# RMS norm on one core: the second tile stored in 4, 4 and 24 rows, the third loaded in one transfer

## The chip, the cores and the metric

The kernel runs on one core of one Trainium2 chip. The metric is the device time of one execution in microseconds (us), here the median of several. The core has engines that work beside each other: TensorE (PE in the profile), VectorE (DVE), ScalarE (ACT), GpSimd (POOL) and SyncE (SP). Each takes its instructions in order and waits on semaphores for the others. Transfers between memory (HBM) and the on-chip memory (SBUF) are issued by an engine's queue, here SP's and ACT's, and are carried out by 16 DMA engines that all queues share. In the profile SP's transfers are q1 and ACT's are q10.

## The reference

```python
def reference(x, gamma):          # x: 16 x 1024 x 512 fp32, gamma: 512 fp32
    eps = 1e-5
    rms = np.sqrt(np.mean(x ** 2, axis=-1, keepdims=True) + eps)
    return (x / rms * gamma).astype(np.float32)
```

There are 16,384 rows of 512 numbers. 33.55 MB are read and 33.55 MB are written, and for each number there is one square, one addition and two multiplications.

## The kernel before

**Tiles.** The rows are cut into four tiles of 4,096. A tile lies on 128 partitions with 32 rows each, so one row of a tile is 2 KB on a partition and 0.26 MB in all, and a whole tile is 64 KB on a partition and 8.39 MB in all. A partition's rows lie one behind the other in HBM too, so a transfer of n rows moves one unbroken run of 2n KB for each partition. There are three slots for tiles: tiles 0, 1 and 2 get slots 0, 1 and 2, and tile 3 uses slot 0 again, so its loads wait until tile 0 has been stored.

**Groups.** Each tile is worked on in two groups of 16 rows, (0, 0), (0, 16), (1, 0) and so on to (3, 16), as the list `groups` has them. In a group ScalarE squares pieces of 7, 5 and 4 rows (7 and 9 in tile 0; line 105) and VectorE sums each piece (line 106). `inverse_rms` makes 1/rms with a square root on ScalarE (line 111) and a reciprocal on VectorE (line 112). GpSimd then scales the last rows of the group (six, seven or three, `share`) and multiplies them by gamma (lines 118 and 119). ScalarE scales the other rows one by one (line 127), and VectorE multiplies these by gamma in one instruction (line 131, in `times_gamma`). The pieces of nine rows in tile 0 put their squares into rows 23 to 31 of slot 2, since nothing has been loaded there yet.

**Order.** The schedule is written by hand: each engine runs its instructions in program order. The loop over `groups` starts each turn with the scaling of the group on GpSimd. Then come the squares and sums of the next group, with ScalarE's row scalings between them, then `times_gamma`, then the stores, and at the end the next group's `inverse_rms`. `transfers_amid` is called at three steps of a turn and issues some loads and stores there; `stores` is called after `times_gamma`.

**Transfers.** SP issues first the loads of tile 0 (in rows 0, 1 to 15 and 16 to 31, with gamma between), then tile 1 whole, then rows 0 to 15 of tile 2. ACT's queue issues rows 16 to 31 of tile 2 in turn (0, 16), and tile 3's two halves in turns (1, 16) and (2, 0). All stores are issued by SP: tile 0 in two halves, which wait until ScalarE has squared seven rows of group (1, 16); tile 1 in two halves in turn (1, 16); tile 2 whole in turn (2, 16); tile 3 in two halves. In `store`, `behind` adds a wait on another instruction. The first store of tile 1 has such a wait on `late[3]`, the load of tile 3's first half, and the second store stands behind it in SP's order.

Of the kernel before, what the change touches and what calls it, by code (L numbers as in the profile page):

```python
# [9 lines left out]
def kernel(  # L10
# [6 lines left out]
    nc = tc.nc  # L17
# [26 lines left out]
    def load(t, slot, r0, r1, queue=nc.sync):  # L44
        dma = queue.dma_start(out=slots[slot][:, r0:r1], in_=xv[t][:, r0:r1])  # L45
        before_scale.append((slot, r0, r1, dma))
        return dma

    def store(t, slot, r0, r1, behind=None):
        dma = nc.sync.dma_start(out=ov[t][:, r0:r1], in_=slots[slot][:, r0:r1])  # L50
        if behind is not None:
            tc.add_manual_dep(
                dma.ins,
                behind.ins.name,
                mybir.DependencyInfo(mybir.DependencyClass.Sync, mybir.DependencyReason.DATA),
                reason="the store is issued when this is done",
            )
        before_scale.append((slot, r0, r1, dma))
# [7 lines left out]
        nc.sync.dma_start(out=gamma_row[:, c0:c1], in_=gamma.unsqueeze(0)[:, c0:c1])  # L66
    load(0, 0, 16, 32)
    load(1, 1, 0, 32)
    load(2, 2, 0, 16)

    ones_col = const.tile([1, P], fp32)
    nc.gpsimd.memset(ones_col, 1.0)  # L72
# [25 lines left out]
    def square_sums(ss, t, g, r, m, k):  # L98
        if m == 9:
            sq = slots[2][:, 23:32, :]  # L100
        else:
            home, name, most = ((psum, "sq_psum", 7), (const, "sq_sbuf", 5))[k % 2]
            sq = home.tile([P, most, D], fp32, name=name)
        rows = slots[slot_of[t]][:, g + r : g + r + m, :]
        squared[t, g + r] = nc.scalar.activation(out=sq[:, :m], in_=rows, func=AF.Square)  # L105
        nc.vector.tensor_reduce(  # L106
            out=ss[:, r : r + m, 0], in_=sq[:, :m], axis=mybir.AxisListType.X, op=OP.add
        )

    def inverse_rms(ss, n):  # L110
        nc.scalar.activation(out=ss[:, :n, 0], in_=ss[:, :n, 0], func=AF.Sqrt, bias=eps_t, scale=1.0 / D)  # L111
        nc.vector.reciprocal(out=ss[:, :n, 0], in_=ss[:, :n, 0])  # L112
        return ss

    def scale_by_pool(rstd, t, g, n, share):
        part = slots[slot_of[t]][:, g + n - share : g + n, :]
        by_row = rstd[:, n - share : n].to_broadcast([P, share, D])
        nc.gpsimd.tensor_tensor(out=part, in0=part, in1=by_row, op=OP.mult)  # L118
        last = nc.gpsimd.tensor_tensor(  # L119
            out=part, in0=part, in1=gamma_b.to_broadcast([P, share, D]), op=OP.mult  # L120
        )
        before_scale.append((slot_of[t], g + n - share, g + n, last))

    def scale(rstd, t, g, r0, r1):
        x = slots[slot_of[t]]
        for r in range(r0, r1):
            nc.scalar.activation(out=x[:, g + r, :], in_=x[:, g + r, :], func=AF.Copy, scale=rstd[:, r])  # L127

    def times_gamma(t, g, r0, r1):
        part = slots[slot_of[t]][:, g + r0 : g + r1, :]  # L130
        scaled = nc.vector.tensor_tensor(  # L131
            out=part, in0=part, in1=gamma_psum.to_broadcast([P, r1 - r0, D]), op=OP.mult
        )
        for slot, b0, b1, earlier in before_scale:
            if slot == slot_of[t] and b0 < g + r1 and g + r0 < b1:
                tc.declare_no_dep(scaled.ins, earlier.ins, reason="ScalarE waited for it before it scaled these rows")

    late = {}

    def transfers_amid(t, g, step):  # L140
        if (t, g, step) == (0, 16, 1):
            load(2, 2, 16, 32, queue=nc.scalar)
        elif (t, g, step) == (1, 0, 0):
            store(0, 0, 0, 16, behind=squared[1, 16])
            store(0, 0, 16, 32)
        elif (t, g, step) == (1, 16, 2):
            late[3] = load(3, 0, 0, 16, queue=nc.scalar)
        elif (t, g, step) == (2, 0, 0):
            load(3, 0, 16, 32, queue=nc.scalar)

    def stores(t, g):
        if (t, g) == (1, 16):
            store(1, 1, 0, 16, behind=late[3])
            store(1, 1, 16, 32)
        elif (t, g) == (2, 16):
            store(2, 2, 0, 32)
        elif t == 3:
            store(3, 0, g, g + 16)

    def pieces_of(group):  # L160
        t, g, n, pieces, share = group
        ss = stats.tile([P, 16, 1], fp32, name="ss")
        r = 0
        todo = []
        for k, m in enumerate(pieces):
            todo.append((ss, t, g, r, m, k))
            r += m
        return ss, todo
# [6 lines left out]
    for k, group in enumerate(groups):  # L175
        t, g, n, pieces, share = group
        mine = n - share
        half = (mine + 1) // 2
        ahead = groups[k + 1 :][:1]
        ss, todo = pieces_of(ahead[0]) if ahead else (None, [])  # L180
        scale_by_pool(rstd, t, g, n, share)
        for piece in todo[:2]:
            square_sums(*piece)
        transfers_amid(t, g, 0)
        scale(rstd, t, g, 0, half)
        transfers_amid(t, g, 1)
        for piece in todo[2:]:
            square_sums(*piece)
        transfers_amid(t, g, 2)
        scale(rstd, t, g, half, mine)  # L190
        times_gamma(t, g, 0, mine)
        stores(t, g)
        for nxt in ahead:
            rstd = inverse_rms(ss, nxt[2])
# [30 lines left out]
```

## Time and profile before

| what | us |
|---|---|
| median of 3 runs (162.65 to 162.98) | 162.69 |
| the profiled execution: its time | 163.35 |
| the profiled execution: its span | 161.2 |
| VectorE busy | 113.1 |
| ScalarE busy | 108.9 |
| GpSimd busy | 102.2 |
| TensorE busy | 2.0 |

The profiled execution's time is 2.15 us over its span, and 0.66 us over the median. Times inside the profile are counted from the start of the span. "Idle before" is time in which an engine had nothing to run, and the name behind it is what ended that time. The DMA share is the busy share of the 16 DMA engines. In a table by stretches a transfer's bytes and time are counted where it starts, so a share can be a little over 1 and the rates of short stretches swing; stretches of 6 us and more are steady.

### The profile page before, as it was taken

How to read it: one execution, taken by the hardware profiler on the slowest of the kernel's cores; microseconds unless marked ns; L12 is line 12 of the kernel's file. 1: busy time of each engine (PE TensorE's matmuls, PEld its weight loads, DVE VectorE, ACT ScalarE, POOL GpSimd, SP SyncE). 2: the span in 40 equal slices, each digit the busy share in tenths (PEclk: the TensorE clock that was granted, in tenths of full speed). 3: DMA queues.
4: the chain of work that ended last, by engine and by line, in shares of the span. 5: the costliest groups of instructions: out<-in, count | busy, mean ns of one | idle time of the engine just before them, and what ended most of it. 6: DMA issues, size and time to landing. Idle time of an engine off the chain costs nothing.

```text
span 161.2 us, 258 instructions
## 1 busy us (share of the span) xinstructions
PE 2.0 (1%) x2; PEld 0.5 (0%) x2; DVE 113.1 (70%) x38; ACT 108.9 (68%) x110; POOL 102.2 (63%) x22
## 2 busy tenths in 40 slices
PE   0005000000000000000000000000000000000000
PEld 0001000000000000000000000000000000000000
DVE  0000992897988999999999999999999801960000
ACT  3007907997599999899989989998995198000000
POOL 1000006993089979999999999999999997000000
DMA  6999999979999999999999999999999699699991
GB/s 204 473 391 463 423 439 472 520 309 472 390 415 488 398 390 455 447 398 447 447 398 407 463 382 423 407 472 423 407 512 504 293 504 504 285 472 423 407 472 57
DMA packets 2163, 67.12 MB, mean 416 GB/s; under 512 B 241, under 2 KB 241, under 8 KB 370
## 3 DMA queue, kind: packets, MB, share of 16 engines
q1 hardware_dynamic: 1730, 54.53, 78.6%
q10 hardware_dynamic: 432, 12.58, 18.7%
q14 instruction: 1, 0.01, 0.0%
HBM read 33.56 MB, written 33.55 MB: 416 GB/s over the span
## 4 chain that ended last, share of the span: by engine, by line
DVE 50%; DMA 25%; ACT 13%; SPq 1%; ACTq 0%; issue 0%
DVE ss L106 27%; DMA slot<-in_x_dram 25%; DVE slot L131 23%; ACT slot L127 8%; ACT sq_psum L105 3%; ACT sq_sbuf L105 1%; SPq L45 1%; DVE ss L112 1%; ACTq L220 0%; SPq L66 0%; ACTq L45 0%
## 5 line engine op out<-in xcount | busy, mean ns | idle before, releaser
L118 POOL TENSOR_TENSOR slot<-slot,ss 128x3584 f32<-128x3584 f32 (+2 forms) x8 | 45.0, 5629 | 32.8 <-DVE ss L112 32.8
L106 DVE TENSOR_REDUCE ss<-sq_psum 128x7 f32<-128x3584 f32 (+1 forms) x14 | 44.5, 3178 | 20.3 <-ACT sq_psum L105 20.3
L119 POOL TENSOR_TENSOR slot<-slot,gamma_b 128x3584 f32<-128x3584 f32 (+2 forms) x8 | 56.9, 7115 | 0.6
L127 ACT ACTIVATE slot<-slot,ss 128x512 f32<-128x512 f32 x77 | 48.5, 707 | 4.7 <-DVE ss L112 4.7
L131 DVE TENSOR_TENSOR slot<-slot,gamma_psum 128x4608 f32<-128x4608 f32 (+2 forms) x8 | 42.2, 5280 | 9.5 <-ACT slot L127 9.5
L105 ACT ACTIVATE sq_psum<-slot 128x3584 f32<-128x3584 f32 (+1 forms) x14 | 36.5, 2604 | 13.8 <-DMA slot<-in_x_dram 13.0
L106 DVE TENSOR_REDUCE ss<-sq_sbuf 128x5 f32<-128x2560 f32 x6 | 16.8, 2803 | 0.0
L105 ACT ACTIVATE sq_sbuf<-slot 128x2560 f32<-128x2560 f32 x6 | 13.9, 2320 | 0.0
L106 DVE TENSOR_REDUCE ss<-slot 128x9 f32<-128x4608 f32 x2 | 9.9, 4952 | 0.1
L105 ACT ACTIVATE slot<-slot 128x4608 f32<-128x4608 f32 x2 | 8.1, 4028 | 0.0
L111 ACT ACTIVATE ss<-ss,eps_t 128x16 f32<-128x16 f32 x8 | 2.4, 304 | 7.8 <-DVE ss L106 7.8
L112 DVE RECIPROCAL ss<-ss 128x16 f32<-128x16 f32 x8 | 2.0, 245 | 0.4 <-ACT ss L111 0.4
L74 PE MATMUL gamma_psum<-gamma_row,ones_col 1*128 1x512 f32 x2 | 2.0, 1122 | 12.6 <-DMA gamma_row<-in_gamma_dram 12.6
L80 ACT ACT_TABLE_LOAD x1 | 1.3, 1283 | 1.2 <-PEq L209 1.2
L174 ACT COPY gamma_b<-gamma_psum 128x512 f32<-128x512 f32 x1 | 0.6, 566 | 0.0
L74 PEld LDWEIGHTS gamma_psum<-gamma_row,ones_col 1*128 1x128 f32 x2 | 0.5, 308 | 12.6 <-issue 12.6
L72 POOL MEMSET ones_col<- 1x128 f32 x1 | 0.2, 194 | 0.3 <-POOLq L209 0.3
L209 POOL MEMSET const-float32-0.0<- 128x1 f32 x1 | 0.1, 99 | 0.2 <-issue 0.2
L80 ACT ACTIVATE table<-eps_t 128x1 f32<-128x1 f32 x1 | 0.2, 203 | 0.0
L209 POOL MEMSET const-bfloat16-1.0<- 128x1 bf16 x1 | 0.1, 102 | 0.0
L209 POOL MEMSET const-uint8-127<- 128x1 uint8 x1 | 0.1, 102 | 0.0
L209 POOL MEMSET const-float32-1.0<- 128x1 f32 x1 | 0.1, 99 | 0.0
(1 smaller groups left out, 0.1 us busy)
## 6 DMA issues: line engine op xcount, KB each, us to landing
out_dram<-slot SPq DMA_DIRECT2D x6, 4096.0 KB, 20.8
slot<-in_x_dram ACTq DMA_DIRECT2D x3, 4096.0 KB, 16.9
slot<-in_x_dram SPq DMA_DIRECT2D x2, 4096.0 KB, 36.5
slot<-in_x_dram SPq DMA_DIRECT2D x1, 3840.0 KB, 11.7
slot<-in_x_dram SPq DMA_DIRECT2D x1, 256.0 KB, 3.0
gamma_row<-in_gamma_dram SPq DMA_DIRECT2D x1, 2.0 KB
slot<-in_x_dram SPq DMA_DIRECT2D x1, 39.6
out_dram<-slot SPq DMA_DIRECT2D x1, 25.1
```

Source lines behind the costliest of these rows:

```text
L45: dma = queue.dma_start(out=slots[slot][:, r0:r1], in_=xv[t][:, r0:r1])
L74: nc.tensor.matmul(gamma_psum[:, 0], ones_col, gamma_row, start=True, stop=True)
L80: nc.scalar.activation(out=table, in_=eps_t, func=AF.Sqrt)
L105: squared[t, g + r] = nc.scalar.activation(out=sq[:, :m], in_=rows, func=AF.Square)
L106: nc.vector.tensor_reduce(out=ss[:, r : r + m, 0], in_=sq[:, :m], axis=mybir.AxisListType.X, op=OP.add)
L111: nc.scalar.activation(out=ss[:, :n, 0], in_=ss[:, :n, 0], func=AF.Sqrt, bias=eps_t, scale=1.0 / D)
L112: nc.vector.reciprocal(out=ss[:, :n, 0], in_=ss[:, :n, 0])
L118: nc.gpsimd.tensor_tensor(out=part, in0=part, in1=by_row, op=OP.mult)
L119: last = nc.gpsimd.tensor_tensor(out=part, in0=part, in1=gamma_b.to_broadcast([P, share, D]), op=OP.mult)
L127: nc.scalar.activation(out=x[:, g + r, :], in_=x[:, g + r, :], func=AF.Copy, scale=rstd[:, r])
L131: scaled = nc.vector.tensor_tensor(out=part, in0=part, in1=gamma_psum.to_broadcast([P, r1 - r0, D]), op=OP.mult)
L174: nc.scalar.copy(out=gamma_b[:, 0], in_=gamma_psum[:, 0])
```

## The change: one load for the third tile, and three stores for the second

Rows 0 to 15 of tile 2 are no longer loaded from SP at the start. The whole tile is loaded by one transfer from ACT's queue, at a new fourth step of turn (0, 0), after the row scalings of that turn; it waits until VectorE has summed the nine squares that lie in slot 2.

Tile 1 is stored in rows 0 to 3 and 4 to 7 in turn (1, 0), right after `times_gamma`, and in rows 8 to 31 in turn (1, 16). The wait on the load of tile 3's first half is gone. No engine's arithmetic changes, neither in kind nor in order.

```diff
-    load(2, 2, 0, 16)
...
-    late = {}
-
     def transfers_amid(t, g, step):
-        if (t, g, step) == (0, 16, 1):
-            load(2, 2, 16, 32, queue=nc.scalar)
+        if (t, g, step) == (0, 0, 3):
+            load(2, 2, 0, 32, queue=nc.scalar)
         elif (t, g, step) == (1, 0, 0):
             store(0, 0, 0, 16, behind=squared[1, 16])
             store(0, 0, 16, 32)
         elif (t, g, step) == (1, 16, 2):
-            late[3] = load(3, 0, 0, 16, queue=nc.scalar)
+            load(3, 0, 0, 16, queue=nc.scalar)
         elif (t, g, step) == (2, 0, 0):
             load(3, 0, 16, 32, queue=nc.scalar)

     def stores(t, g):
-        if (t, g) == (1, 16):
-            store(1, 1, 0, 16, behind=late[3])
-            store(1, 1, 16, 32)
+        if (t, g) == (1, 0):
+            store(1, 1, 0, 4)
+            store(1, 1, 4, 8)
+        elif (t, g) == (1, 16):
+            store(1, 1, 8, 32)
         elif (t, g) == (2, 16):
             store(2, 2, 0, 32)
...
         times_gamma(t, g, 0, mine)
+        transfers_amid(t, g, 3)
         stores(t, g)
```

## The prediction

> **What bounds the kernel now.** I read the table by stretches first, for the DMA share and rate are what 67 MB must pass through.
>
> ```profile
> DMA packets 2163, 67.12 MB, mean 416 GB/s; under 512 B 241, under 2 KB 241, under 8 KB 370
> ...
> 56.00:62.00 6.00, 0.00 (x0) 0.00 (x0) 6.00 (x3) 6.00 (x6) 4.92 (x2) 1.00 0.98 404
> 62.00:78.00 16.00, 0.00 (x0) 0.00 (x0) 16.00 (x7) 14.99 (x17) 15.92 (x3) 1.00 1.01 438
> 78.00:84.00 6.00, 0.00 (x0) 0.00 (x0) 6.00 (x3) 5.44 (x7) 5.92 (x2) 1.00 0.99 415
> ...
> 92.00:98.00 6.00, 0.00 (x0) 0.00 (x0) 6.00 (x3) 5.44 (x7) 5.92 (x2) 1.00 1.03 404
> 98.00:156.00 58.00, 0.00 (x0) 0.00 (x0) 37.36 (x13) 32.35 (x39) 37.92 (x7) 1.00 1.00 434
> ```
>
> The last two columns are DMA share and GB/s. The DMA engines are full from 4 to 158 us, for loads, stores and both mixed, at about 434 GB/s: 27.1 on each of 16 engines, 1.21 us for a 32 KB transfer. 67.12 MB at 434 is 154.7 us; start (2 us) and the time after the last data make up most of the rest. Three stretches are slower. By the records of single transfers the loss is 0.25 us at 58 to 61 (loads in flight get slow as tile 0's stores join), 0.24 at 80 to 83 (loads of tile 3 take over from stores) and 0.57 at 94 to 96 (two stores of tile 1 join the loads; each engine's load of 1.21 us takes 1.6 to 1.9).
>
> Next, the DMA view of the last 4 us, in slices of 0.1 us:
>
> ```profile
> GB/s 655 655 328 655 0 328 655 0 0 0 0 0 0 0 0 0 0 0 328 0 0 0 0 0 0 0 0 0 0 0 0 0 0 0 0 0 0 0 0 0
> ```
>
> A 328 is one 32 KB transfer starting. The last one starts at 158.8, over 1 us behind the rest: fifteen engines end at 158.07 to 158.89, one at 160.05, and the span ends with it. By the records that engine ended its last tile-0 store at 80.42 and got its first tile-3 load only at 81.47; at the end of the load's first half it is 1.2 us behind (91.70 against 90.50) and stays so. So in this execution the bound is one engine's queue run dry once.
>
> Then the timeline, for when transfers are issued and needed:
>
> ```profile
> 32.94 4.95 DVE L106 TENSOR_REDUCE ss<-slot 128x9 f32<-128x4608 f32 x1
> ...
> 41.96 3.16 ACT L105 ACTIVATE sq_psum<-slot 128x3584 f32<-128x3584 f32 x1 [2.73 <-DMA slot<-in_x_dram]
> 44.76 0.39 ACTq L45 DMA_DIRECT2D slot<-in_x_dram  x1
> ...
> 58.00 3.93 SPq L50 DMA_DIRECT2D out_dram<-slot  x2
> 68.42 4.94 DVE L131 TENSOR_TENSOR slot<-slot,gamma_psum 128x4608 f32<-128x4608 f32 x1
> 77.36 0.33 ACTq L45 DMA_DIRECT2D slot<-in_x_dram  x1
> 82.28 0.33 ACTq L45 DMA_DIRECT2D slot<-in_x_dram  x1
> 92.17 51.73 SPq L50 DMA_DIRECT2D out_dram<-slot  x5
> 96.12 3.14 ACT L105 ACTIVATE sq_psum<-slot 128x3584 f32<-128x3584 f32 x1
> 109.81 3.14 ACT L105 ACTIVATE sq_psum<-slot 128x3584 f32<-128x3584 f32 x1
> 136.41 7.09 DVE L131 TENSOR_TENSOR slot<-slot,gamma_psum 128x6656 f32<-128x6656 f32 x1 [8.14 <-ACT slot L127]
> ```
>
> Tile 3's halves land at 92.04 and 108.4 and are squared from 96.12 and 109.81. The last store is issued at 143.6, but its data runs from 148.5: 4.9 us of queue lies before it. The chain of waits ends in VectorE's line 131, but a compute delay of some 2 us would not be felt at the end.
>
> **The change part by part.**
>
> *Load of tile 2.* SP issues one transfer less at 2.9 (0.45 us, beside running transfers: nothing). ACT's queue issues the whole tile, waiting for the nine-row sum that ends at 32.94 + 4.95 = 37.89. The queue runs ahead of the engine (the load at 44.76 was issued with scalings pending until 50.44), so I put the issue at 37.95. Behind it stands the square root of line 111, which waits for the same sum and started at 38.94; the issue's 0.39 us ends at 38.34, so nothing moves. The issue at 44.76 goes: nothing, ScalarE had work. What is new is that q1 runs dry when tile 1 is in, at 41.02 to 41.56 by engine. From issue to an engine's first transfer it took at least 2.6 us at 58.00 and 77.36, where a queue took over, and 4.1 on the late engine. So the load is ready at 40.55 to 42.05: no hole on most engines, up to 1.0 us on a late one. I take 0.3; ends 0 and 1.0. It can't get in front of tile 1's last transfers, which start by 39.14. Tile 2 is in at some 61, needed at 68.75.
>
> *Stores of rows 0 to 3 and 4 to 7.* Issued when line 131 ends, at 73.36, on an SP that was waiting 30.1 us for the load. They queue behind tile 0 on q1, which drains at 79.98 to 80.74. There the hole of the late engine closes, since q1 has work: 1.16 us (160.05 less 158.89) on the profiled execution. The runs' median is 0.66 under it, so they may lack it; I take 0.4, ends 0 and 1.16.
>
> *Sharing.* Where two queues have 32 KB transfers, each engine alternates one by one (98 to 104 us). With 8 KB against 32 KB a pair takes 0.31 + 1.21 = 1.52 us and loads keep 80%. Each engine has 8 + 8 small stores and 8 + 8 load transfers, so both queues finish together: tile 3's halves end at 80.3 + 8 x 1.52 = 92.5 and 104.7, before 96.12 and 109.81. No wait appears. Rows 8 to 31 need GpSimd's line 119, to 87.95; they are issued at 88.0, run when the small ones are out and end at 104.7 + 14.5 = 119.2, much as now.
>
> *Cost of small transfers.* 2 KB ones took 0.084 us at the start (24.4 GB/s) and 32 KB ones 1.21 (27.0). Between them, 8 KB costs 0.309 for 0.303: 16 x 0.006 = +0.1 us. The upper end is the slowest 8 KB records before the span, 0.361: +0.9.
>
> On 1 MB transfers the Trainium skill says more (DMA: Bandwidth & Descriptors, section Bandwidth): 6.15 us for 1 MB, 78% of peak. By that, an estimate from the page, the two small stores (1.05 MB each) would take 12.3 us instead of 4.8 and lose up to 7.5; by this trace, where queued transfers follow without a hole (434 GB/s from 98 to 156), 0.1. I hold with the row: the rule's figure is for a transfer alone.
>
> *The join at 94.* Two stores on an empty q1 become one on a queue already running. Stores added to a running q1 (116, 130, 143.6) slowed nothing, but no loads ran then. Ends: -0.57 and 0. I take -0.3. The join at 58 stays.
>
> Sum: +0.3 - 0.4 + 0.1 - 0.3 = -0.3 on the profiled 163.35; the same -0.3 on the median of 162.69 gives 162.39. With the join gone wholly it is 162.1. I say 162.25, between.
>
> **The rivals.**
>
> *No change.* DMA was and is full, and the gains are a few tenths: the join stays, the late engine was in the profile only, and the small transfers cost what they may. 162.4 to 163.0. For it: 434 GB/s everywhere. Against: three slow stretches, of which two are touched.
>
> *A new hole at 41 us (slower).* If ACT's queue issues only after its ten scalings (end 39.03), the load is ready at 41.7 to 43.2, against 41.02 to 41.56: 0.2 to 2 us lost, no work to fill it. It decides from an issue after 38.9. Less the gains: 163.1 to 164.2. Against: the issue at 44.76.
>
> *Small transfers as bad company (slower).* If an engine gives a queue several small transfers a turn, loads fall under 63% (4.19 MB by 95.7) from 2.4 a turn on. At four, equal bytes, tile 3's halves come at 100 and 119; ScalarE is 10 us late at the end, and the last store, issued at 153.8, makes 168.8. A mere pause of 0.1 to 0.24 us at each of 16 small transfers (the slowest 2 KB record less the usual, 0.32 - 0.084, is the upper end) would make 163.8 to 166. The trace has no mixed sizes.
>
> **How the numbers follow.** About 0.2% (0.33 us) is what a measurement here can tell from no change. Chances: my forecast 0.47 (161.3 to 162.36, the low end with the late engine's hole and the join both gone: 162.69 - 1.16 - 0.57 + 0.3 = 161.3); no change 0.22; hole 0.18; company 0.13. The likeliest case's own range is 161.3 to 162.36. 161.3 to 163.7 holds the first two and over half of the third, about 0.8. Faster 0.47, same 0.22, slower 0.31.
>
> **What would show it.** ACT's load of tile 2 issued at 38.0, with q10's first data by 41.6; small stores issued at 73.4, alternating with loads 1 to 4 in bytes; tile 3's halves landing near 93 and 105; no 404 stretch at 92 to 98; all engines ending within 1 us; ScalarE's squares at 96.1 and 109.8. A load issued after 38.9, a wait of ScalarE on a load after 90, or a rate under 420 between 80 and 105 would make it wrong.

## The result: 169.83 us, 4% slower

The changed kernel takes 169.83 us (median of 4 runs, 169.35 to 169.94) against 162.83 us (4 runs) for the kernel before: a ratio of 1.0424 with a 95% interval of 1.0398 to 1.0449. I had forecast 162.25 us and a range up to 163.7. In the profiled execution (169.35 us) the span grew from 161.2 to 167.2 us. In `kernel.py` the lines of the arithmetic are one lower than before (the square is line 104, the sum 105, the gamma product 130).

### The profile after

The waits of the changed kernel (total us, number of times, longest):

```profile
POOL slot L117 <- DVE ss L111: 43.0, 5, 24.7
DVE ss L105 <- ACT sq_psum L104: 31.0, 8, 16.1
ACT sq_psum L104 <- DMA slot<-in_x_dram: 26.0, 4, 10.2
```

The line of ScalarE's squares before:

```profile
ACT sq_psum L105 <- DMA slot<-in_x_dram: 13.0, 2, 10.3
```

Before, ScalarE's squares waited for loads twice, 13.0 us in all. Now it is four times and 26.0 us, and the waits of VectorE and GpSimd follow from that. The timeline names the four places (the first, 10.2 us, is the start of the program):

```profile
37.83 0.38 ACTq L45 DMA_DIRECT2D slot<-in_x_dram  x1
...
44.30 3.16 ACT L104 ACTIVATE sq_psum<-slot 128x3584 f32<-128x3584 f32 x1 [5.16 <-DMA slot<-in_x_dram]
...
60.33 30.33 SPq L50 DMA_DIRECT2D out_dram<-slot  x5
...
79.69 0.33 ACTq L45 DMA_DIRECT2D slot<-in_x_dram  x1
...
101.58 3.16 ACT L104 ACTIVATE sq_psum<-slot 128x3584 f32<-128x3584 f32 x1 [3.03 <-DMA slot<-in_x_dram]
...
122.14 3.16 ACT L104 ACTIVATE sq_psum<-slot 128x3584 f32<-128x3584 f32 x1 [7.64 <-DMA slot<-in_x_dram]
...
148.15 7.09 DVE L130 TENSOR_TENSOR slot<-slot,gamma_psum 128x6656 f32<-128x6656 f32 x1 [8.13 <-ACT slot L126]
```

ScalarE starts on tile 1 at 44.30 instead of 41.96, waits 3.03 us for tile 3's first half and 7.64 us for its second. So the last product ends at 155.24 instead of 143.50. The table by stretches shows what that does to the DMA engines (last columns: DMA share and GB/s):

```profile
36.00:60.00 24.00, 0.00 (x0) 0.00 (x0) 19.30 (x7) 18.84 (x20) 15.71 (x3) 1.00 1.01 437
...
82.00:88.00 6.00, 0.00 (x0) 0.00 (x0) 6.00 (x3) 5.44 (x7) 5.92 (x2) 1.00 1.05 370
...
98.00:118.00 20.00, 0.00 (x0) 0.00 (x0) 17.80 (x7) 13.23 (x14) 19.92 (x3) 1.00 1.00 433
118.00:150.00 32.00, 0.00 (x0) 0.00 (x0) 17.33 (x8) 20.99 (x26) 20.37 (x5) 1.00 0.99 429
151.10:156.00 4.90, 0.00 (x0) 0.00 (x0) 4.14 (x1) 0.00 (x0) 0.00 (x0) 1.00 0.00 0
```

Before, 98 to 156 us was full at 434 GB/s. Now nothing moves from 151.0 to 156.1: everything else has been stored, and the last 4.19 MB wait for VectorE. That is 5.1 of the 6.0 us. By the records of single transfers, 0.4 us more is lost than before at 58 to 64, 1.0 at 80 to 88, 0.1 at 94 to 98 and 0.4 in small dips; the late engine's 1.2 us at the end of the span before is gone (all sixteen end within 0.2 us, having all started again together after the 5.1 us stop). Together 5.1 + 0.4 + 1.0 + 0.1 + 0.4 - 1.2 = 5.8.

### Where the delay is made

The DMA view of the changed kernel at the end of tile 1's load, from 41.0 to 41.6 us (all packets; then by queue packets, MB and share of 16 engines):

```profile
DMA packets 27, 1.05 MB, mean 1748 GB/s; under 512 B 11, under 2 KB 11, under 8 KB 11
...
q10 hardware_dynamic: 16, 1.05, 406.2%
q1 hardware_dynamic: 11, 0.00, 1.0%
```

The same view from 43.0 to 44.2 us:

```profile
DMA packets 21, 1.05 MB, mean 874 GB/s; under 512 B 5, under 2 KB 5, under 8 KB 5
...
q10 hardware_dynamic: 16, 1.05, 201.5%
q1 hardware_dynamic: 5, 0.00, 0.2%
```

A load ends with one note of 4 bytes from each of the 16 engines, and ScalarE needs all 16. Tile 1's data is in on every engine by 41.46. On 11 engines the note follows at once (41.02 to 41.45). Once both queues are running, an engine takes one transfer from one and then one from the other (the counts further down); I call that a queue's turn. On five engines the other queue's first 64 KB transfer gets the turn between data and note, and the note comes at 43.69 to 43.80, one turn of 2.42 us later. The Trainium skill (DMA: Bandwidth & Descriptors, section Why a DMA increments its semaphore by 16 and not by 1) says that each engine's last descriptor is the increment and that only the full 16 means landed; this trace agrees, 11 + 5 notes, and adds that another queue's transfer can come before the note.

Then the sharing. The DMA view of the changed kernel from 86 to 94 us (q10 is loads, q1 stores):

```profile
q10 hardware_dynamic: 86, 2.82, 85.6%
q1 hardware_dynamic: 86, 0.67, 19.8%
```

And from 98 to 118 us:

```profile
q1 hardware_dynamic: 112, 5.51, 63.5%
q10 hardware_dynamic: 112, 3.15, 36.4%
```

In both, packet stands against packet, 86 to 86 and 112 to 112. So beside 8 KB stores the 32 KB loads move four fifths of the bytes (2.82 of 3.49 MB), and beside the 24-row store (48 KB) 36% (3.15 of 8.65 MB). By the records, 16 of the 112 on q10 are not data but the notes of tile 3's first half: each comes right after a 48 KB transfer of q1, at 99.06 to 101.20. So here too a note has to wait for its turn. By the records, q1 starts the small stores at 80.7, tile 3's first load starts at 84.6, and by then 10.7 of the 16 small stores of an engine are gone. The loads have had 7.1 of their 16 turns when the 48 KB turns begin at 96; the last nine take until 121.8.

### The profile page after: what moved, and what is told of

It is laid out like the page before. It is cut to its first block, busy times and chain, and to the rows that moved or that the text cites. A ratio compares the mean times of both kernels' runs of the same rounds, so it can differ in the third digit from the quotient of the medians.

```text
span 167.2 us, 258 instructions
## 1 busy us (share of the span) xinstructions
PE 2.0 (1%) x2; PEld 0.5 (0%) x2; DVE 113.8 (68%) x38; ACT 108.7 (65%) x110; POOL 102.2 (61%) x22
## 4 chain that ended last, share of the span: by engine, by line
DMA 47%; DVE 24%; ACT 20%; SPq 1%; ACTq 0%; issue 0%
DMA slot<-in_x_dram 47%; DVE slot L130 13%; ACT slot L126 11%; DVE ss L105 10%; ACT sq_psum L104 6%; ACT sq_sbuf L104 3%; SPq L45 1%; ACTq L220 0%; DVE ss L111 0%; SPq L66 0%; ACT ss L110 0%
## 5 line engine op out<-in xcount | busy, mean ns | idle before, releaser
L73 PE MATMUL gamma_psum<-gamma_row,ones_col 1*128 1x512 f32 x2 | 2.0, 1119 | 12.9 <-DMA gamma_row<-in_gamma_dram 12.9
L73 PEld LDWEIGHTS gamma_psum<-gamma_row,ones_col 1*128 1x128 f32 x2 | 0.5, 308 | 12.9 <-issue 12.9
```

The costliest lines, as they stand in the source:

```text
L73: nc.tensor.matmul(gamma_psum[:, 0], ones_col, gamma_row, start=True, stop=True)
```

## The experiments

The change has two parts, and the two places above suggest two theories: the late note of tile 1 ("overtaking" in the expectations below, which I wrote before I had looked at the notes) and the 48 KB turn ("turn"). The first four runs part them.

**1. The load alone.** The kernel before with tile 2 loaded whole:

```diff
-    load(2, 2, 0, 16)
...
-        if (t, g, step) == (0, 16, 1):
-            load(2, 2, 16, 32, queue=nc.scalar)
+        if (t, g, step) == (0, 0, 3):
+            load(2, 2, 0, 32, queue=nc.scalar)
...
         times_gamma(t, g, 0, mine)
+        transfers_amid(t, g, 3)
```

> The kernel before with one part of the change: tile 2 is loaded whole from ACT's queue in turn (0, 0); the stores of tile 1 stay as they were, behind the load of tile 3's first half. Theory 'turn' (the loss is made where the 24-row store, 48 KB a transfer, shares the DMA engines with tile 3's loads of 32 KB): tile 1 lands late by about 2.3 us as in the changed kernel, a hole of about 0.5 us opens at 60 us, and the queue before the last store hides the rest: 162.9 to 163.8 us. Theory 'overtaking' (the loss comes from tile 2's load getting in front of tile 1's last transfers): the late start alone makes most of the 7 us: 167 us or more.

Measured: 163.95 us against 162.63, ratio 1.0066 (1.0047 to 1.0086). ScalarE starts on tile 1 at 44.41 (15 notes by 41.65, one at 43.92: one is enough). No load is waited for after that, and the last product starts at 138.86, 2.4 us late, with the queue still full. This part alone costs about 1 us and not 7, a little more than the theory "turn" had it.

**2. The stores alone.** The kernel before with tile 1 stored in 4, 4 and 24 rows:

```diff
-        if (t, g) == (1, 16):
-            store(1, 1, 0, 16, behind=late[3])
-            store(1, 1, 16, 32)
+        if (t, g) == (1, 0):
+            store(1, 1, 0, 4)
+            store(1, 1, 4, 8)
+        elif (t, g) == (1, 16):
+            store(1, 1, 8, 32)
```

> The kernel before with the other part alone: tile 1 stored in 4, 4 and 24 rows that wait for no load; tile 2 is loaded as it was. Theory 'turn': tile 3's second half lands at 118 to 121 us instead of 108.4, ScalarE waits 2 to 4 us for the first half and 6 to 9 us for the second, the last store is issued at 152 to 155 us, the queue is dry for 3 to 5 us before it: 166.5 to 168.5 us. Theory 'overtaking': tile 1 lands at 42, no lasting loss: 162.5 to 163.5 us.

Measured: 162.37 us against 162.63, ratio 0.9985 (0.9966 to 1.0003): no difference that can be told. The theory "turn" fails as I had put it. The timeline says why:

```profile
77.41 0.33 ACTq L45 DMA_DIRECT2D slot<-in_x_dram  x1
...
96.16 3.14 ACT L105 ACTIVATE sq_psum<-slot 128x3584 f32<-128x3584 f32 x1
...
114.24 3.16 ACT L105 ACTIVATE sq_psum<-slot 128x3584 f32<-128x3584 f32 x1 [4.30 <-DMA slot<-in_x_dram]
...
140.25 7.09 DVE L131 TENSOR_TENSOR slot<-slot,gamma_psum 128x6656 f32<-128x6656 f32 x1 [8.13 <-ACT slot L127]
```

In this timeline of the run with the stores alone, tile 3's load is issued at 77.41, only 4.9 small stores an engine are gone at its first transfer, and it gets 12.7 of its 16 turns before the 48 KB turns begin. Its second half comes 4.30 us late, and the last product ends at 147.34, before the queue has run out: its store's first data starts at 148.26, and no gap opens. So each part alone costs about 1 us or nothing (ratios 1.0066 and 0.9985), and both together 1.0424: the loss is made by the two meeting.

**3. No 48 KB turn.** The changed kernel with the 24 rows in six stores of four:

```diff
-            store(1, 1, 8, 32)
+            for r in range(8, 32, 4):
+                store(1, 1, r, r + 4)
```

> The changed kernel with rows 8 to 31 of tile 1 stored in six transfers of four rows (8 KB a partition) instead of one of 24 rows (48 KB); same rows, same moment. Theory 'turn': loads keep 80% of the DMA engines, tile 3's halves land near 96 and 108 us, ScalarE waits for neither over 1 us: 162.7 to 164 us. Theory 'overtaking': no change, 169 to 170 us. Theory 'small transfers' (8 KB transfers themselves slow the DMA engines): four times as many of them, 171 us or more.

Measured: 163.62 us against 162.63, ratio 1.0043 (1.0016 to 1.007). Tile 1's note is still late (44.45) and 10.3 small stores an engine are still gone before the first load, but the loads end at 109.8 and ScalarE waits for neither half. Four times as many 8 KB transfers did not make it slower, as the theory "small transfers" had it.

**4. No late note.** The changed kernel with tile 2's whole load on SP's queue:

```diff
-            load(2, 2, 0, 32, queue=nc.scalar)
+            load(2, 2, 0, 32)
```

> The changed kernel with tile 2's whole load issued by SP instead of ACT, so that it stands behind tile 1's load on one queue and can't overtake it. Theory 'turn': tile 1 lands at 42.0 instead of 44.3 us and ScalarE's squares begin there, but tile 3's second half still lands after 118 us: 167 to 169 us. Theory 'overtaking': 162.5 to 163.5 us.

Measured: 162.75 us against 162.63, ratio 1.0008 (0.9983 to 1.0033).

```profile
41.98 3.16 ACT L104 ACTIVATE sq_psum<-slot 128x3584 f32<-128x3584 f32 x1 [2.75 <-DMA slot<-in_x_dram]
```

The load is issued at the same moment as in the changed kernel (37.92), and only its queue differs. ScalarE starts on tile 1 at 41.98, tile 3's second half is waited for 4.60 us, as in run 2, and the loss is gone. So taking away either the late note or the 48 KB turn takes away 6 to 7 us.

**The theory after these four: used-up cover.** The late note makes all computing 2.3 us late. ACT issues tile 3's load by that much later, but SP's small stores stand in their queue all the same and run on. They are the only stores that leave the loads four fifths; when they have gone, the 48 KB turns take over. Its rival is that the 2.3 us are simply added to the wait that run 2 has.

**5. The load of tile 3 late, with nothing else late.** Run 2 with that load held until a sum of VectorE's that ends at 80.0:

```diff
-        elif (t, g, step) == (1, 16, 2):
+        elif (t, g, step) == (1, 16, 3):
             late[3] = load(3, 0, 0, 16, queue=nc.scalar)
+            tc.add_manual_dep(late[3].ins, summed[2, 7].ins.name, ...)
...
-        nc.vector.tensor_reduce(
+        summed[t, g + r] = nc.vector.tensor_reduce(
...
         times_gamma(t, g, 0, mine)
+        transfers_amid(t, g, 3)
```

> Tile 1 in 4, 4 and 24 rows and tile 2's load as before (as in the run with the stores alone, 162.37 us), but the load of tile 3's first half waits for a sum that VectorE ends at 80.0, so that it is issued some 2.5 us later than there, beside a q1 that has not moved. No computing is delayed by it, nothing overtakes. Theory 'used-up cover' (the 7 us come from tile 3's load arriving when most of the small stores have gone, so that the 24-row store takes 60% beside the loads for longer): the second half lands at 119 to 123 us, ScalarE waits 9 to 13 us for it, 166 to 170 us. Theory 'late computing' (what the changed kernel loses is the 2.3 us by which computing is late, added to the wait that the 24-row store makes): 162.3 to 163.5 us.

Measured: 168.55 us against 162.74, ratio 1.0351 (1.0315 to 1.0387). Its timeline:

```profile
42.03 3.16 ACT L106 ACTIVATE sq_psum<-slot 128x3584 f32<-128x3584 f32 x1 [2.73 <-DMA slot<-in_x_dram]
...
80.14 0.33 ACTq L45 DMA_DIRECT2D slot<-in_x_dram  x1
...
103.12 3.16 ACT L106 ACTIVATE sq_psum<-slot 128x3584 f32<-128x3584 f32 x1 [6.83 <-DMA slot<-in_x_dram]
121.15 3.16 ACT L106 ACTIVATE sq_psum<-slot 128x3584 f32<-128x3584 f32 x1 [5.10 <-DMA slot<-in_x_dram]
```

Tile 1 is on time, yet 2.7 us at one issue (77.41 to 80.14) cost 6 us: 12.9 small stores an engine are gone, 5.8 loads have had their turn, ScalarE waits 6.83 and 5.10 us (I had put the whole wait on the second half), and the DMA engines stand from 151.0 to 155.2. Late computing can't be the cause here, since none was late before these waits.

**6. Half the turn before the note.** The changed kernel with tile 2 in two loads of 32 KB a partition:

```diff
-            load(2, 2, 0, 32, queue=nc.scalar)
+            load(2, 2, 16, 32, queue=nc.scalar)
+            load(2, 2, 0, 16, queue=nc.scalar)
```

> The changed kernel with tile 2 loaded from ACT's queue at the same moment in two halves (32 KB a partition) instead of one transfer (64 KB). If a transfer of the new queue gets in front of tile 1's last transfer on an engine, it costs one turn: 1.2 us instead of 2.4, so tile 1 lands at 43.0 to 43.3 instead of 44.3 us. Theory 'used-up cover': tile 3's load is issued 1.2 us earlier than in the changed kernel, about 4 small stores an engine more are left to go beside it, the second half lands at 116 to 119 us: 164 to 167 us. If instead the whole wait of tile 1 doesn't follow the size of the turn: tile 1 at 44.3 us and 169 to 170 us.

Measured: 167.13 us (the median of its three fastest executions, 166.22, 167.13 and 168.45; the fourth took 168.75) against 162.74, ratio 1.0276 (1.0221 to 1.0331); the profiled execution took 166.22.

```profile
43.10 3.16 ACT L104 ACTIVATE sq_psum<-slot 128x3584 f32<-128x3584 f32 x1 [1.06 <-DMA slot<-in_x_dram]
...
119.08 3.16 ACT L104 ACTIVATE sq_psum<-slot 128x3584 f32<-128x3584 f32 x1 [8.04 <-DMA slot<-in_x_dram]
```

Thirteen notes come by 41.54 and three at 42.63 to 42.68: the delay is one turn, now of 1.21 us, and ScalarE starts at 43.10 as expected. The median is 0.1 us over the range. By the ratios, 1.0276 against 1.0424, half the lag cost about two thirds of the loss.

The runs with the 48 KB store side by side (small stores and loads are of 16 on an engine, counted in the records; the dry time is that before the last store):

| run | small stores gone at the first load | loads before the first 48 KB turn | last load data, us | ScalarE's waits for tile 3, us | DMA dry, us | median, us |
|---|---|---|---|---|---|---|
| load 2 on SP | 3.9 | 13.7 | 112.3 | 0, 4.60 | 0 | 162.75 |
| stores alone | 4.9 | 12.7 | 112.1 | 0, 4.30 | 0 | 162.37 |
| load 2 in halves | 5.9 | 11.8 | 116.9 | 0, 8.04 | 3.5 | 167.13 |
| the change | 10.7 | 7.1 | 121.8 | 3.03, 7.64 | 5.1 | 169.83 |
| late load 3 | 12.9 | 5.8 | 120.8 | 6.83, 5.10 | 4.1 | 168.55 |

**7. The wait put back.** The changed kernel with the 24-row store behind tile 3's first half:

```diff
+    late = {}
...
-            load(3, 0, 0, 16, queue=nc.scalar)
+            late[3] = load(3, 0, 0, 16, queue=nc.scalar)
...
-            store(1, 1, 8, 32)
+            store(1, 1, 8, 32, behind=late[3])
```

> The changed kernel with one edit: the 24-row store waits for the load of tile 3's first half, as the store of tile 1 did in the kernel before. Tile 2's load still overtakes tile 1's and the small stores are still used up early. Theory 'used-up cover': tile 3's first half lands at 95 to 98 us, the 24-row store starts its data near 100 instead of 94 us, the second half lands at 111 to 115, ScalarE waits 0 to 3 us: 163.2 to 165.2 us. If the order of the 24-row store and the loads is not what costs: 168 us or more.

Measured: 164.25 us against 162.49, ratio 1.0118 (1.0099 to 1.0137). The first 48 KB turn comes at 101.6, after 12.0 loads; ScalarE waits 4.78 us for the second half, which is more than I expected, and the last store is issued at 150.2, about when the queue ends. The wait that the change removed is worth about 5 us beside the late note (ratios 1.0118 and 1.0424).

**8. What is left of the load's cost.** Run 1 with tile 0's first store issued at 54.7 instead of 60.5 us, to fill the gap between tile 2's load and that store:

```diff
-            store(0, 0, 0, 16, behind=squared[1, 16])
+            store(0, 0, 0, 16, behind=squared[1, 12])
```

> The run with tile 2's whole load on ACT's queue alone (163.95 us, 1.3 over its kernel before), with one edit: tile 0's first store waits for the last four squared rows of group (1, 0) instead of seven rows of group (1, 16), so that it is issued near 54.6 instead of 60.5 us, while tile 2's load still runs. If the hole at 60 to 62 us (0.7 us of DMA time) makes most of the 1.3 us: 162.6 to 163.3 us and no stretch under 380 GB/s at 60 to 62. If the loss lies in the slow stretch at 80 to 84 us: 163.6 to 164.2 us.

Measured: 164.52 us against 162.49, ratio 1.0154 (1.011 to 1.0198). The expectation failed. The gap is gone, but by the records the DMA engines now move 350 to 370 GB/s from 56 to 62 us and lose 1.1 us from 56 to 64, against 0.8 in run 1. The records place what run 1 loses: 0.8 us at 56 to 64, 1.0 at 80 to 88 and 0.9 at 94 to 98, against 0.3, 0.25 and 0.6 in the kernel before. Why the same places cost more there is left open.

**9 and 10. Versions that might be better.** All of tile 1 in fours, with tile 2 loaded as before:

```diff
-        if (t, g) == (1, 16):
-            store(1, 1, 0, 16, behind=late[3])
-            store(1, 1, 16, 32)
+        if (t, g) == (1, 0):
+            store(1, 1, 0, 4)
+            store(1, 1, 4, 8)
+        elif (t, g) == (1, 16):
+            for r in range(8, 32, 4):
+                store(1, 1, r, r + 4)
```

> The kernel before with tile 1 stored in eight transfers of four rows that wait for no load; tile 2 is loaded as before. Loads keep 80% beside all of tile 1's stores, so tile 3's halves land near 95 and 107 us and ScalarE waits for neither: 162.0 to 162.6 us. If 8 KB transfers cost more than their bytes: above 162.8 us.

Measured: 162.29 us against 162.74, ratio 0.9995 (0.9965 to 1.0026): the same as before. ScalarE waits for neither half of tile 3. The other version has every transfer on SP's queue:

```diff
-            load(2, 2, 16, 32, queue=nc.scalar)
+            load(2, 2, 16, 32)
...
-            late[3] = load(3, 0, 0, 16, queue=nc.scalar)
-        elif (t, g, step) == (2, 0, 0):
-            load(3, 0, 16, 32, queue=nc.scalar)
+            load(3, 0, 0, 16)
+            load(3, 0, 16, 32)
...
-            store(1, 1, 0, 16, behind=late[3])
+            store(1, 1, 0, 16)
```

> The kernel before with every load and store on SP's queue, in the order of need: tile 2's second half, tile 0's stores, tile 3's two halves, tile 1's stores (no wait on a load), tile 2's store, tile 3's stores. One queue is one order: nothing overtakes, nothing is shared, no queue takes over from another. Tile 3's halves land near 90.5 and 100.5 us, all of tile 1 is stored after them, ScalarE waits for no load after 42 us. If the slow stretches of the kernel before (58 to 61, 80 to 83, 94 to 96, 1 us together, and a dry engine at 80) come from two queues joining or taking over, they go: 161.0 to 162.2 us. If they come from loads and stores meeting in the DMA engines on any queue: 162.4 to 163.0 us.

Measured: 161.96 us against 162.74, ratio 0.9954 (0.9927 to 0.998): 0.5% faster than the kernel before, the best of the study. The table by stretches of this run:

```profile
56.00:62.00 6.00, 0.00 (x0) 0.00 (x0) 6.00 (x3) 6.00 (x5) 4.91 (x2) 1.00 0.97 393
...
78.00:84.00 6.00, 0.00 (x0) 0.00 (x0) 6.00 (x3) 5.44 (x7) 5.92 (x2) 1.00 1.02 437
...
92.00:98.00 6.00, 0.00 (x0) 0.00 (x0) 6.00 (x3) 5.44 (x7) 5.92 (x2) 1.00 1.01 437
98.00:104.00 6.00, 0.00 (x0) 0.00 (x0) 6.00 (x3) 6.00 (x6) 6.00 (x2) 1.00 1.07 431
```

Where loads follow stores (78 to 84) 415 GB/s has become 437. Where stores follow loads, the dip at 56 to 62 stays (393), and by the records the one at 94 to 96 has moved to 98 to 102, where tile 1's stores now begin (353 and 415 GB/s in two slices of 2 us). So the first and third of the three slow stretches lie where stores begin after loads, on one queue as on two; only the second is gone. The time fell into the range of the first theory although two of its three stretches stayed, so the number is in part luck. The second stretch is worth 0.2 us by the records. Nor does this run show that the change of queue alone removed it, for tile 3's first load is also issued earlier (71.80 instead of 77.36).

## Why the prediction was wrong

- **Load of tile 2, issue and hole: right.** Issued at 37.83 (37.95 forecast), first data at 41.02 to 41.46, no hole between the loads.
- **"It can't get in front of tile 1's last transfers": the first step that failed.** It was true of the data and false of the landing. In the profile before each note comes right behind its data (16 records of 4 bytes at 41.02 to 41.56), since no other queue was running then, and I took the last data's end for the landing. Five notes of 4 bytes took their turn behind 64 KB, and ScalarE was 2.3 us late.
- **"A compute delay of some 2 us would not be felt at the end": right for the place that I looked at, wrong as a price.** In run 1 the last store's queue hid it. But the delay also moves the issue of tile 3's load against stores that now wait for nothing, which I didn't follow.
- **Sharing, "both queues finish together": the step that cost most.** I let small stores and loads begin together at 80.3. The stores begin when q1 gets to them (80.7). The load's data starts 3.7 to 4.9 us after its issue where q1 goes on working (78.51 to 82.22 in run 6; 77.41 to 81.36 in run 2; 79.69 to 84.63 here), not 2.6 as at the two places where a queue took over. Nor is 2.6 a least time: in run 1 a load had its first data 1.0 us after its issue (79.82 to 80.80), when q1 ran out. Why a working q1 holds the load back so long isn't shown. Even with tile 1 on time the second half ended at 112.1 and not at 104.7, and ScalarE waited 4.3 us ("no wait appears"). With tile 1 late it was 121.8.
- **"Rows 8 to 31 run when the small ones are out": right, but priced as harmless.** It would be harmless with the loads in; with nine of 16 still to come, each load of 1.21 us stood beside a 48 KB transfer of 1.82 us, so they came two and a half times as slowly as alone.
- **The late engine's hole: closed, and worth nothing that can be told.** I took 0.4 us off. The profile of the stores alone ends without a late engine, yet its median is no lower than before by more than the measurement can tell (0.9985).
- **Small transfers: right.** In steady alternation 8 KB took 0.309 us. When the loads joined, 52 of the 256 took over 0.35 us and the stretch from 82 to 88 fell to 370 GB/s, which I had not priced. The 78% that the Trainium skill gives for 1 MB transfers (DMA: Bandwidth & Descriptors, section Bandwidth) was measured on loads issued by GpSimd, and the page doesn't say that they ran alone, as I took it. It is not seen for the queued stores here: eight of 1 MB in run 9 changed the time by a ratio of 0.9995.
- **The join at 94: wrong.** I took 0.3 us off; 0.67 was lost at 94 to 98 against 0.56 before (my 0.57 was of these 4 us, and not of 94 to 96). In the one-queue run the loss moved to where tile 1's stores begin, so it may go with stores that follow loads; the cause isn't shown.
- **The rivals.** "Bad company" named the place (tile 3's loads losing their share) and, for equal bytes, a time near the measured one (168.8), with 0.13 for both its forms. Its reason was wrong: the 8 KB stores kept to a fifth, and the 48 KB store took the share. That its time came near is luck: it let equal bytes go on for all 16 load turns, while at four a turn the 16 small stores of an engine would be gone after four. The upper end of the pause was misread too: the slowest 2 KB record in the profile before took 0.605 us, not 0.32. A hole at 41 us didn't appear.

## What to carry to other kernels

In these runs two DMA queues shared the engines by turns and not by bytes (86 packets to 86, 112 to 112), so a transfer's bytes per partition set its queue's share (8 KB against 32 KB left the loads 80%, 48 KB left them 36%), and stores with small runs protect loads only as long as they last. A wait that looks idle can be what keeps a large transfer out of the way of one that is needed sooner: before removing it, ask what happens when the other queue is 2 us later than in the trace. Where DMA is full all along, one queue in order of need has neither turns nor late notes, and here it was the fastest (161.96 us, ratio 0.9954).

## What the runs showed of the hardware that I had not expected

- A load is complete only with its notes, and a note waits for its turn like any transfer: 2.42 us behind 64 KB (run 1 and the change), 1.82 behind 48 KB (the change, at 99 to 101), 1.21 behind 32 KB (run 6). One late engine of 16 is enough (run 1).
- The DMA engines lose 0.3 to 0.6 us where stores begin after loads, on two queues (the kernel before) or on one (run 10), and 0.7 to 1.1 us in runs 1 and 8.
- From the issue of tile 3's first load to its first data it took 1.0 us (run 1) to 4.9 us (the change), longest beside a q1 that had work. The cause isn't shown.
- The engine that ran dry at 80 us in the profile before closed the span 1.2 us late there. Three of the versions without that gap (runs 2, 4 and 9) have spans of 160.1 us, yet the medians of the stores alone and of all fours differ from before by less than the measurement can tell.
